# Residual added in PSUM: seeding the accumulation banks of a feed-forward block from ScalarE

## The chip, the cores and the metric

The kernel runs on one core of one Trainium2 chip. The metric is the device time in microseconds (us) of one execution; the times here are the median of three runs of the kernel before, and one further execution that was taken with the hardware profiler on.

## What is computed

The reference is a small decoder trunk over 512 tokens of width 1024, in two layers. Each layer is a feed-forward block (FFN), a mixer (gated linear attention, GLA, in the first layer; stick-breaking attention, SB, in the second), and another FFN, so there are four FFNs in all:

```
x = x + 0.5 * (silu(h @ w_gate) * (h @ w_up)) @ w_down      # h = rmsnorm(x); D_FF = 2816
x = x + mixer(rmsnorm(x))
x = x + 0.5 * (the same with the second FFN's weights)
```

The change concerns the FFNs alone: the additions of `0.5 * (...) @ w_down` to the residual `x`, and the way in which part of the gate and up products are formed.

## The kernel before

**Layout and precision.** The residual stays on the chip as eight tiles `xs[0..7]` of 128 features by 512 tokens. Every matrix factor is held as two parts, a rounded one (`wh`, `hh`, `nh` and so on) and a remainder (`wl`, `hl`, `nl`); one product is three matmuls, high by high, low by high and high by low (`mm3`, line 89; `prod`, line 523). A weight block is loaded by SyncE, rounded by ScalarE (line 133, called a cast here) and subtracted from the original by VectorE (line 134, the remainder).

**The order of the work.** The whole kernel is one list of entries (`Entry`, `Feed`, lines 116 to 178). When an entry starts, `Feed.start` first writes down the casts and remainders of the entries up to two further on, and then the entry's own body. That order of the code counts later: between two instructions of an engine that could both run, the one written first goes first. The weight halves `wh` and `wl` have four buffers each, so that a cast waits for TensorE to finish with a block.

**An FFN.** The hidden width is cut into eleven column pairs, collected in six groups (`GROUPS`, line 449). The first gate and up products are plain (`feat`, line 183). From the third or fourth column pair on, gate and up products are formed by the seven-product scheme of `seven` (line 503): 8 gate and 9 up products in each FFN, 32 and 36 in the kernel, 68 in all; each is called a seven here. A seven has two entries. `body_1` runs four products and `body_2` three, each of 12 matmuls of 256 columns. In the order of TensorE they are

```
body_1:  w   z   q   w+=          body_2:  y   q+=   o
```

where `w`, `z`, `q` are left halves of three PSUM banks and `y`, `o` are the right halves of the banks of `z` and `w`. The sums between products are made on the way out: ScalarE copies `w` to `u2` (line 563) and `q` to `c5` (line 570); VectorE adds `z` to `u2` (line 566), `y` to `u2` to give `u3` (line 582), `u3` to `c5` (line 583), `q` to `u2` (line 586) and `o` to `u3` (line 591). All of `add` is recorded at line 539. `left` and `rest` (lines 541 to 553) then apply the silu on ScalarE (gate) or multiply by the finished gate on VectorE (up), and `close` splits the result in `hh` and `hl` for the down projection.

**Down.** `down` (line 292) multiplies a group's hidden columns by `w_down`. For each of the eight feature blocks k it accumulates `nf` hidden blocks in one PSUM bank `ps_d` (12 matmuls of 512 columns for `nf` = 4; 6 for the fifth group, which has `nf` = 2), and VectorE takes `0.5 * ps_d + x` to `x` (line 308). Entries of `down` for a group are placed between the sevens of the next group, mostly two feature blocks at a time (four for the fifth group). In the steady part one `body_1`, one `body_2` and one entry of `down` follow each other. After the sixth group, `nxt` prepares the next norm; in the last FFN the sixth group is done by `back_tok` instead. So 5 groups × 8 blocks × 4 FFNs = 160 additions are within an FFN, and 24 are in the sixth groups.

**Banks.** PSUM has eight banks, under the tags a (2), z (3), t (2) and o (1). A call of `psum` without a tag takes the next of `aazzztto` in turn (line 45).

Of the kernel before, what the change touches and what calls it, by code (L numbers as in the profile page):

```python
# [14 lines left out]
AF = mybir.ActivationFunctionType  # L15
ALU = mybir.AluOpType
# [3 lines left out]
T = 512  # L20
D = 1024
KD = D // P
# [8 lines left out]
def decoder(ctx: ExitStack, tc: tile.TileContext, a: dict, out: bass.AP):  # L31
    nc = tc.nc
# [10 lines left out]
    turn_ = [0]  # L43

    def psum(name, tag=None):
        if tag is None:
# [12 lines left out]
    xs = [xp.tile([P, T], F32, name=f"x{k}") for k in range(KD)]  # L59

    def mm(ps, l, r, first, last):
        st["pe"] = nc.tensor.matmul(ps, l, r, start=first, stop=last).ins  # L62

# [16 lines left out]
    def back_by(ps, u):  # L80
        return ps.rearrange("p (m u) -> p u m", u=u)

    def like(x, u):
        return x.rearrange("p (u m) -> p u m", u=u)

    def mm2(ps, l, r, first, last):
        mm(pairs(ps), l, two(r), first, last)

    def mm3(ps, wh, wl, mh, ml, first, last, o=pairs, m=two):
        ps, mh, ml = o(ps), m(mh), m(ml)  # L90
        mm(ps, wh, mh, first, False)
        mm(ps, wl, mh, False, False)
        mm(ps, wh, ml, False, last)
# [89 lines left out]
    def feat(ch, f, evac, tag=None, defer=None, part=KD // 2, o=pairs, m=two):  # L183


        def body(W):
            (wh, wl), = W
            ps = psum("ps_f", tag)
            for ks in (range(0, part), range(part, KD)):
                for k in ks:  # L190
                    mm3(ps, wh[:, k], wl[:, k], st["h"][k], st["l"][k], k == 0, k == KD - 1, o, m)
                if ks[-1] == KD - 1:
                    if defer is None:
                        evac(ps)
# [31 lines left out]
    def back(w, r0, nf, hs, scale, nxt, late=0, tags=(None,) * 8):  # L226


        for dh in range(2):
# [45 lines left out]
            for f0, u in units:  # L275
# [13 lines left out]

                feed.q.append(Entry([u], body))  # L290

    def down(w, r0, nf, hs, part, nxt):

        nd = KD // nf
        src = w[r0 : r0 + nf * P, part * nd * P : (part + 1) * nd * P]
        ch = Chunk(src.rearrange("(f p) c -> p f c", p=P), nf, nd * P)
        ch.few = True

        def body(W):
            (wh, wl), = W  # L300
            for m in range(nd):
                ps = psum("ps_d")
                s = slice(m * P, (m + 1) * P)
                for f in range(nf):
                    mm3(ps, wh[:, f, s], wl[:, f, s], hs[f][0], hs[f][1], f == 0, f == nf - 1)
                k = part * nd + m
                x = like(xs[k], 4)
                nc.vector.scalar_tensor_tensor(  # L308
                    out=x, in0=back_by(ps, 4), scalar=0.5, in1=x, op0=ALU.mult, op1=ALU.add
                )  # L310
                if nxt is not None:
                    nxt(k)
                yield

        feed.q.append(Entry([(ch, lambda t: t, nf, nd * P)], body))
# [26 lines left out]
    st = {}  # L342
# [99 lines left out]
    class FFN:  # L442
# [10 lines left out]
        def __init__(self, wg, wu, wd, gi, nxt, first=False, last=False):  # L453
# [6 lines left out]
            for group, (c0, c1) in enumerate(self.GROUPS):  # L460
# [29 lines left out]
                for x in downs[put:]:  # L490
                    down(*x)
# [4 lines left out]
            if last:  # L496
                back_tok(wd, c0 * 256, n, self.hs[group], nxt)
            else:
                for x in downs:
                    down(*x)  # L500
            self.total = len(feed.q) - base

        def seven(self, ch, group=None):

            H = T // 2
            s12, v = [None], {}

# [12 lines left out]
            def prod(o, w, w0, b, first=True):  # L523
                for j in range(4):
                    bh, bl = b(j)
                    wh, wl = w[0][:, w0 + j], w[1][:, w0 + j]
                    for n, (l_, r_) in enumerate(((wh, bh), (wl, bh), (wh, bl))):
                        nc.tensor.matmul(  # L528
                            pairs(o), l_, r_, start=first and j + n == 0, stop=j == 3 and n == 2, skip_group_check=True
                        )  # L530

            def half(k0, c):
                return lambda j: (four(st["h"][k0 + j])[:, c], four(st["l"][k0 + j])[:, c])

            def part(name):
                return self.tp.tile([P, H], F32, tag="c", bufs=2, name=name)

            def add(o, x, y):
                nc.vector.tensor_tensor(out=o, in0=x, in1=y, op=ALU.add)  # L539

            def left(o, w):
                if group is None:
                    nc.scalar.activation(o[:, 0:H], w, AF.Silu)
                else:
                    nc.vector.tensor_tensor(out=o[:, 0:H], in0=w, in1=self.gates[0][:, 0:H], op=ALU.mult)

            def rest(o, c):
                if group is None:
                    st["silu"] = nc.scalar.activation(o[:, c:T], o[:, c:T], AF.Silu).ins
                    self.gates.append(o)  # L550
                    return
                nc.vector.tensor_tensor(out=o[:, c:T], in0=o[:, c:T], in1=self.gates.pop(0)[:, c:T], op=ALU.mult)
                self.close(o, group)

            def body_1(W):
                ax, s = W

                v["w"], v["z"], v["q"] = psum("ps_w"), psum("ps_z"), psum("ps_q")
                w, z, q = (v[n][:, 0:H] for n in "wzq")
                v["o"] = self.tp.tile([P, T], F32, tag="t", name="o0")  # L560
                prod(w, ax, 0, half(0, 0))
                v["u2"] = part("u2")
                nc.scalar.copy(v["u2"], w)
                yield
                prod(z, s, 4, lambda j: self.t_half(1, j))
                add(v["u2"], z, v["u2"])
                yield
                prod(q, s, 0, lambda j: self.t_half(0, j))
                v["c5"] = part("c5")
                nc.scalar.copy(v["c5"], q)  # L570
                yield
                prod(w, ax, 4, half(4, 0), first=False)
                left(v["o"], w)
                yield

            def body_2(W):
                s, a22 = W
                q, y = v["q"][:, 0:H], v["z"][:, H:T]
# [672 lines left out]
    with tc.tile_pool(name="ip", bufs=1) as ip:  # L1251
# [95 lines left out]
        ps = psum("ps_g")  # L1347
# [51 lines left out]
```

## Time and profile before

| | |
|---|---|
| median of 3 runs | 1829.39 us (1829.24 to 1830.08) |
| profiled execution, own time | 1829.62 us |
| its span, first to last instruction | 1827.8 us |
| TensorE busy | 1794.6 us (98%) |
| VectorE busy | 1454.1 us (80%) |
| ScalarE busy | 935.9 us (51%) |
| granted TensorE clock | 0.997 |
| chain that ended last | PE 82%, DVE 10%, ACT 4%, DMA 3% |

In the profile PE is TensorE's matmul, PEld its weight load, DVE VectorE, ACT ScalarE, POOL GpSimd and SP SyncE. A row of a group shows line, engine and operation, output and inputs by the kernel's names, shape and count; then total busy time, the mean ns of one, and the idle time of the engine just before them with what ended it. A row of the timeline shows start in us from the span's start, duration, engine, line, and in brackets the engine's idle time before it and the releaser. A matmul's duration is its whole passage, so successive matmuls overlap; the distance of their starts is the rate.

### The profile page before, as it was taken

Reading aid. Unit: us, or ns where it says so; the run is one execution under the profiler, and the core shown is the slowest. Engines: PE = TensorE matmul, PEld = TensorE weight load, DVE = VectorE, ACT = ScalarE, POOL = GpSimd, SP = SyncE. Lnnn points to the kernel's source line nnn. Section 1 sums busy time; section 2 is a strip of 40 time slices with the busy share of each in tenths; the row PEclk is TensorE's granted clock in tenths of the full one; section 3 lists DMA queues with packets and bytes.
Section 4 is the critical chain, followed back from the end, with each engine's and each line's share of the span. In section 5 each row is a group of like instructions: output and inputs, shape, how many; then the busy total and the mean of one; then the engine's idle time right before and its main releaser. Section 6 shows DMA issues by size and latency. Waiting matters only on the chain.

```text
span 1827.8 us, 28865 instructions
## 1 busy us (share of the span) xinstructions
PE 1794.6 (98%) x11790; PEld 1642.5 (90%) x11790; DVE 1454.1 (80%) x2311; ACT 935.9 (51%) x1450; POOL 7.3 (0%) x17
## 2 busy tenths in 40 slices
PE   7999999999999999999999999999999999999998
PEld 6899999889988899999989999999888788999997
DVE  5987878775776988887889878777878769888785
ACT  5544444543664544444464444445888855444344
POOL 0000000100000000000000000000000000000000
PEclk9999999999999999999999999999999999999999
DMA  5333332322123333333234233223222222333321
GB/s 162 101 119 104 106 126 82 113 70 70 47 70 102 107 115 105 104 116 105 81 109 134 86 122 105 92 94 104 70 64 64 67 95 93 127 105 104 117 92 69
DMA packets 177511, 179.01 MB, mean 98 GB/s; under 512 B 4034, under 2 KB 167924, under 8 KB 177380
## 3 DMA queue, kind: packets, MB, share of 16 engines
q1 hardware_dynamic: 176192, 175.13, 29.7%
q8 instruction: 92, 1.51, 0.3%
q0 software_dynamic: 512, 0.99, 0.2%
q10 hardware_dynamic: 676, 1.07, 0.2%
q14 instruction: 39, 0.32, 0.1%
HBM read 175.11 MB, written 2.10 MB: 97 GB/s over the span
## 4 chain that ended last, share of the span: by engine, by line
PE 82%; DVE 10%; ACT 4%; DMA 3%; issue 1%; SPq 0%; ACTq 0%; DVEq 0%
PE ps_d L62 24%; PE ps_w L528 14%; PE ps_f L62 12%; PE ps_z L528 9%; PE ps_q L528 9%; PE ps_t L62 4%; PE ps_b L62 3%; DVE wl L134 2%; PE ps_S L62 1%; DMA raw<-in_ffn_w_up_dram 1%; PE ps_bt L62 1%; ACT wh L133 1%; PE ps_oT L1141 1%; PE ps_z L1079 1%; ACT l L439 1%
## 5 line engine op out<-in xcount | busy, mean ns | idle before, releaser
L134 DVE TENSOR_TENSOR wl<-raw,wh 128x1024 fp32r<-128x1024 f32 x244 | 261.9, 1073 | 68.2 <-ACT wh L133 67.2
L133 ACT CAST wh<-raw 128x1024 fp32r<-128x1024 f32 x244 | 225.4, 927 | 120.9 <-PE ps_f L62 42.0
L62 PE MATMUL ps_d<-hh,wh 128*128 128x512 f32 x672 | 255.0, 379 | 0.0
L62 PE MATMUL ps_d<-hl,wh 128*128 128x512 f32 x672 | 254.8, 379 | 0.0
L62 PE MATMUL ps_d<-hh,wl 128*128 128x512 f32 x672 | 254.8, 379 | 0.0
L133 ACT CAST wh<-s 128x1024 fp32r<-128x1024 f32 x136 | 142.3, 1046 | 131.9 <-PE ps_q L528 76.8
L62 PE MATMUL ps_f<-xh,wh 128*128 128x512 f32 x448 | 177.2, 396 | 5.2 <-ACT wh L133 3.7
L134 DVE TENSOR_TENSOR wl<-s,wh 128x1024 fp32r<-128x1024 f32 x136 | 166.0, 1222 | 17.8 <-ACT wh L133 16.5
L308 DVE SCALAR_TENSOR_TENSOR x<-ps_d,x 128x512 f32<-128x512 f32 x184 | 125.2, 689 | 64.5 <-PE ps_d L62 64.5
L62 PE MATMUL ps_f<-xh,wl 128*128 128x512 f32 x448 | 170.8, 381 | 0.5 <-DVE wl L134 0.5
L62 PE MATMUL ps_f<-xl,wh 128*128 128x512 f32 x448 | 170.5, 381 | 0.0
L133 ACT CAST wh<-rawd 128x1024 fp32r<-128x1024 f32 x84 | 88.0, 1048 | 136.1 <-PE ps_d L62 115.1
L528 PE MATMUL ps_z<-th,wh 128*128 128x256 f32 x544 | 150.2, 276 | 3.1 <-DVE u L539 3.1
L528 PE MATMUL ps_w<-nh,wl 128*128 128x256 f32 x544 | 149.7, 275 | 0.0
L528 PE MATMUL ps_z<-tl,wh 128*128 128x256 f32 x544 | 149.7, 275 | 0.0
L528 PE MATMUL ps_w<-nl,wh 128*128 128x256 f32 x544 | 149.7, 275 | 0.0
L528 PE MATMUL ps_z<-th,wl 128*128 128x256 f32 x544 | 149.7, 275 | 0.0
L528 PE MATMUL ps_w<-nh,wh 128*128 128x256 f32 x544 | 149.6, 275 | 0.0
L62 PEld LDWEIGHTS ps_d<-hl,wh 128*128 128x128 f32 x672 | 127.1, 189 | 17.9
L62 PEld LDWEIGHTS ps_d<-hh,wh 128*128 128x128 f32 x672 | 127.3, 189 | 16.5
L62 PEld LDWEIGHTS ps_d<-hh,wl 128*128 128x128 f32 x672 | 127.3, 189 | 16.4
L134 DVE TENSOR_TENSOR wl<-rawd,wh 128x1024 fp32r<-128x1024 f32 x84 | 102.8, 1224 | 38.3 <-ACT wh L133 38.0
(250 smaller groups left out, 4707.1 us busy)
## 6 DMA issues: line engine op xcount, KB each, us to landing
raw<-in_ffn_w_gate_dram SPq DMA_DIRECT2D x43, 1024.0 KB, 5.2
raw<-in_ffn_w_up_dram SPq DMA_DIRECT2D x43, 1024.0 KB, 5.2
rawd<-in_ffn_w_down_dram SPq DMA_DIRECT2D x84, 512.0 KB, 3.4
raw<-in_gla_w_in_dram SPq DMA_DIRECT2D x12, 1024.0 KB, 5.2
raw<-in_sb_w_in_dram SPq DMA_DIRECT2D x16, 512.0 KB, 3.7
raw<-in_gla_w_out_dram SPq DMA_DIRECT2D x4, 1024.0 KB, 4.9
raw<-in_sb_w_in_dram SPq DMA_DIRECT2D x4, 1024.0 KB, 5.0
raw<-in_sb_w_out_dram SPq DMA_DIRECT2D x4, 1024.0 KB, 4.9
```

Of the source, the lines that this page charges most:

```text
L62: st["pe"] = nc.tensor.matmul(ps, l, r, start=first, stop=last).ins
L133: nc.scalar.copy(h, r).ins,
L134: nc.vector.tensor_tensor(out=l, in0=r, in1=h.bitcast(F32), op=ALU.subtract).ins,
L308: nc.vector.scalar_tensor_tensor(out=x, in0=back_by(ps, 4), scalar=0.5, in1=x, op0=ALU.mult, op1=ALU.add)
L439: st["last"] = nc.scalar.activation(o, i, fn, **kw).ins
L528: nc.tensor.matmul(pairs(o), l_, r_, start=first and j + n == 0, stop=j == 3 and n == 2, skip_group_check=True)
L1079: nc.tensor.matmul(o_, l_, r_, start=first, stop=last, skip_group_check=True)
L1141: nc.tensor.matmul(po[e * 64 : e * 64 + 64, j * P : T], self.v[j][:, c : c + 64], self.wt[p, e][bk][:, c0 : c0 + n], start=j == 0, stop=j ...
```

## The change

Three things are done.

- `down`, in the first five groups of an FFN: before the matmuls of block k, ScalarE writes twice the residual, `2 * x`, in the bank (`seed`). The matmuls add to it, none of them with the start flag. ScalarE reads the bank back at half scale, `x = 0.5 * ps`, in place of VectorE's multiply-and-add. The seed of block k+1 is written down after the first of the `nf` hidden blocks of block k; that of block 0 at the head of the group's first entry. The sixth group keeps the old way.
- Banks: `down` uses the two banks with tag a alone; the sevens use the other six in the order `zzztto`. The rest still goes through `aazzztto`.
- `seven`: ScalarE copies the first product `w` into the bank of `z`, and four products are added there one after the other, with ScalarE and VectorE reading the sum in between. The order on TensorE becomes

```
body_1:  w   q   z+=   w+=        body_2:  z+=   q+=   z+=
```

with ScalarE's copy of `w` to `z` after the first, of `q` to `c5` after the second, of `z` to `u2` after the third; and VectorE's `z + c5` after the first product of `body_2`. Three VectorE additions of each seven go (`u2`, `u3`, and `o` to `u3`).

```diff
+        if tag == "s":
+            tag = "zzztto"[turn_[1] % 6]
+            turn_[1] += 1
...
+        def seed(k):
+            seeds[k] = psum("ps_d", "a")
+            nc.scalar.activation(
+                seeds[k].rearrange("p (m u) -> p m u", u=4),
+                xs[k].rearrange("p (u m) -> p m u", u=4),
+                AF.Copy,
+                scale=2.0,
+            )
+
         def body(W):
             (wh, wl), = W
+            if nxt is None and part == 0:
+                seed(0)
             for m in range(nd):
-                ps = psum("ps_d")
+                k = part * nd + m
                 s = slice(m * P, (m + 1) * P)
+                seeded = nxt is None
+                ps = seeds.pop(k) if seeded else psum("ps_d", "a")
                 for f in range(nf):
-                    mm3(ps, wh[:, f, s], wl[:, f, s], hs[f][0], hs[f][1], f == 0, f == nf - 1)
-                k = part * nd + m
+                    mm3(ps, wh[:, f, s], wl[:, f, s], hs[f][0], hs[f][1], not seeded and f == 0, f == nf - 1)
+                    if seeded and f == 0 and k + 1 < KD:
+                        seed(k + 1)
                 x = like(xs[k], 4)
-                nc.vector.scalar_tensor_tensor(
-                    out=x, in0=back_by(ps, 4), scalar=0.5, in1=x, op0=ALU.mult, op1=ALU.add
-                )
-                if nxt is not None:
+                if seeded:
+                    nc.scalar.activation(x, back_by(ps, 4), AF.Copy, scale=0.5)
+                else:
+                    nc.vector.scalar_tensor_tensor(
+                        out=x, in0=back_by(ps, 4), scalar=0.5, in1=x, op0=ALU.mult, op1=ALU.add
+                    )
                     nxt(k)
...
                 prod(w, ax, 0, half(0, 0))
-                v["u2"] = part("u2")
-                nc.scalar.copy(v["u2"], w)
-                yield
-                prod(z, s, 4, lambda j: self.t_half(1, j))
-                add(v["u2"], z, v["u2"])
+                nc.scalar.copy(z, w)
                 yield
                 prod(q, s, 0, lambda j: self.t_half(0, j))
                 v["c5"] = part("c5")
                 nc.scalar.copy(v["c5"], q)
                 yield
+                prod(z, s, 4, lambda j: self.t_half(1, j), first=False)
+                v["u2"] = part("u2")
+                nc.scalar.copy(v["u2"], z)
+                yield
                 prod(w, ax, 4, half(4, 0), first=False)
                 left(v["o"], w)
...
-                prod(y, s, 0, lambda j: self.t_half(2, j))
-                u3 = o1[:, 0:H]
-                add(u3, y, v["u2"])
-                nc.vector.tensor_tensor(out=o1[:, H:T], in0=u3, in1=v["c5"], op=ALU.add)
+                prod(z, s, 0, lambda j: self.t_half(2, j), first=False)
+                add(o1[:, H:T], z, v["c5"])
                 yield
                 prod(q, s, 4, half(4, 1), first=False)
                 add(o0[:, H:T], q, v["u2"])
                 rest(o0, H)
                 yield
-                o = v["w"][:, H:T]
-                prod(o, a22, 0, lambda j: self.t_half(3, j))
-                add(o1[:, 0:H], o, u3)
-                rest(o1, 0)
+                prod(z, a22, 0, lambda j: self.t_half(3, j), first=False)
+                left(o1, z)
+                rest(o1, H)
                 yield
```

More of the change, by code (lines that the diff above doesn't have):

```diff
@@ L42, in decoder @@
     order = "aazzztto"
-    turn_ = [0]
+    turn_ = [0, 0]
     def psum(name, tag=None):
-        if tag is None:
+        if tag == "s":
+            tag = "zzztto"[turn_[1] % 6]
+            turn_[1] += 1
+        elif tag is None:
             tag = order[turn_[0] % 8]
@@ L61, in mm @@
     def mm(ps, l, r, first, last):
-        st["pe"] = nc.tensor.matmul(ps, l, r, start=first, stop=last).ins
+        st["pe"] = nc.tensor.matmul(ps, l, r, start=first, stop=last, skip_group_check=True).ins
     def two(m):
@@ L290, in back @@
                 feed.q.append(Entry([u], body))
+    seeds = {}
     def down(w, r0, nf, hs, part, nxt):
@@ L556, in body_1 @@
                 ax, s = W
-                v["w"], v["z"], v["q"] = psum("ps_w"), psum("ps_z"), psum("ps_q")
-                w, z, q = (v[n][:, 0:H] for n in "wzq")
+                v["w"], v["z"], v["q"] = (psum(n, "s")[:, 0:H] for n in ("ps_w", "ps_z", "ps_q"))
+                w, z, q = (v[n] for n in "wzq")
                 v["o"] = self.tp.tile([P, T], F32, tag="t", name="o0")
                 prod(w, ax, 0, half(0, 0))
-                v["u2"] = part("u2")
-                nc.scalar.copy(v["u2"], w)
-                yield
-                prod(z, s, 4, lambda j: self.t_half(1, j))
-                add(v["u2"], z, v["u2"])
+                nc.scalar.copy(z, w)
                 yield
@@ L577, in body_2 @@
                 s, a22 = W
-                q, y = v["q"][:, 0:H], v["z"][:, H:T]
+                q, z = v["q"], v["z"]
                 o0, o1 = v["o"], self.tp.tile([P, T], F32, tag="t", name="o1")
-                prod(y, s, 0, lambda j: self.t_half(2, j))
-                u3 = o1[:, 0:H]
-                add(u3, y, v["u2"])
-                nc.vector.tensor_tensor(out=o1[:, H:T], in0=u3, in1=v["c5"], op=ALU.add)
+                prod(z, s, 0, lambda j: self.t_half(2, j), first=False)
+                add(o1[:, H:T], z, v["c5"])
                 yield
```

## The prediction

> **What bounds the kernel now.** I read the page first, then the groups of instructions by form, TensorE's waits, and at last the timeline of two neighbouring sevens in the steady part of the first FFN.
>
> ```profile
> span 1827.8 us, 28865 instructions
> PE 1794.6 (98%) x11790; PEld 1642.5 (90%) x11790; DVE 1454.1 (80%) x2311; ACT 935.9 (51%) x1450; POOL 7.3 (0%) x17
> PEclk9999999999999999999999999999999999999999
> ```
>
> TensorE is busy for 98% at the full granted clock. The change keeps every matmul, so only TensorE's waits can be won. Those that end in the instructions that the change touches are two lines of the waits:
>
> ```profile
> PE ps_z L528 <- DVE u L539: 3.1, 5, 1.4
> PE ps_w L528 <- DVE o L545: 0.7, 2, 0.3
> ```
>
> That is 3.1 + 0.7 = 3.8 us in the whole kernel, and it bounds the gain. VectorE at 80% looks like a load worth lifting, but almost nobody waits for it here. So the question is which new waits TensorE gets.
>
> **Engine time moved.** The rows that price it:
>
> ```profile
> L308 DVE SCALAR_TENSOR_TENSOR x<-ps_d,x 128x512 f32<-128x512 f32 x184 | 125.2, 689 | 64.5 <-PE ps_d L62 64.5
> L539 DVE TENSOR_TENSOR u<-ps_z,u 128x256 f32<-128x256 f32 x68 | 28.6, 421 | 11.1 <-PE ps_z L528 11.1
> L563 ACT COPY u<-ps_w 128x256 f32<-128x256 f32 x68 | 25.3, 372 | 18.5 <-PE ps_w L528 18.5
> L1228 ACT ACTIVATE ps_bt<-x 128x512 f32<-128x512 f32 x8 | 4.8, 602 | 8.2 <-DVE x L1223 8.2
> L1150 ACT CAST oh<-ps_oT 128x512 fp32r<-128x512 f32 x8 | 4.7, 586 | 10.4 <-PE ps_oT L1141 10.4
> ```
>
> VectorE loses 160 × 0.689 = 110 us of residual additions and 3 × 68 × 0.421 = 86 us of half-width additions: 1454 − 196 = 1258 us, 69%. (The last `left` and `rest` of a seven work on two halves instead of one whole, which moves either engine by some 5 us and is left out.) ScalarE gains 160 seeds at 0.602 (the nearest row that writes a bank), 160 read-backs at 0.586 (one that reads a bank) and 68 copies at 0.372: 190 + 25 = 215, so 936 + 215 = 1151 us, 63%. Neither becomes the bound by its total. What decides is the order of reads and writes in one bank.
>
> **The seven, the new wait.** In `body_2` the three products are now z+=, q+=, z+=. VectorE must read z between the first and the third, so it has as long as the second takes. Before, the same read (`u3`, of y) stood at the same place of the code, and nobody waited for it: the third product went to another bank. So the trace shows when VectorE gets there. An up seven, then a gate seven, on TensorE (first matmul of `body_2`, last of its first product, first of its third):
>
> ```profile
> 206.28 0.28 PE L528 MATMUL ps_z<-th,wh 128*128 128x256 f32 x1
> ...
> 207.51 0.28 PE L528 MATMUL ps_z<-tl,wh 128*128 128x256 f32 x1
> ...
> 208.96 0.28 PE L528 MATMUL ps_w<-th,wh 128*128 128x256 f32 x1
> ...
> 222.07 0.28 PE L528 MATMUL ps_z<-tl,wh 128*128 128x256 f32 x1
> ...
> 223.52 0.28 PE L528 MATMUL ps_w<-th,wh 128*128 128x256 f32 x1
> ```
>
> and on VectorE:
>
> ```profile
> 206.55 1.22 DVE L134 TENSOR_TENSOR wl<-raw,wh 128x1024 fp32r<-128x1024 f32 x1 [0.21 <-ACT wh L133]
> 207.69 0.42 DVE L545 TENSOR_TENSOR o<-ps_w,o 128x256 f32<-128x256 f32 x1
> 208.03 1.22 DVE L134 TENSOR_TENSOR wl<-s,wh 128x1024 fp32r<-128x1024 f32 x1
> 209.16 0.42 DVE L539 TENSOR_TENSOR o<-ps_z,u 128x256 f32<-128x256 f32 x1
> ...
> 221.22 1.22 DVE L134 TENSOR_TENSOR wl<-raw,wh 128x1024 fp32r<-128x1024 f32 x1
> 222.39 1.23 DVE L134 TENSOR_TENSOR wl<-s,wh 128x1024 fp32r<-128x1024 f32 x1
> 223.53 0.42 DVE L539 TENSOR_TENSOR o<-ps_z,u 128x256 f32<-128x256 f32 x1
> ```
>
> In the up seven the first product is complete at 207.51 + 0.28 = 207.79, but at 208.03 VectorE takes a remainder of 1.22 us, because the code writes the next seven's split ahead of this body. The read ends at 209.16 + 0.42 = 209.58, while the third product started at 208.96. With both on one bank the third product waits. How long a restart takes is shown by the one large wait of this kind:
>
> ```profile
> 162.03 0.42 DVE L539 TENSOR_TENSOR u<-ps_z,u 128x256 f32<-128x256 f32 x1
> 162.50 0.38 PE L528 MATMUL ps_z<-th,wh 128*128 128x256 f32 x1 [1.42 <-DVE u L539]
> ```
>
> 162.50 − 162.45 = 0.05. So the up seven would wait 209.58 + 0.05 − 208.96 = 0.67 us, the gate seven 223.53 + 0.42 + 0.05 − 223.52 = 0.48.
>
> Does VectorE, relieved, get there earlier? The two remainders come when ScalarE has cast, and that hangs on TensorE:
>
> ```profile
> 205.20 0.37 ACT L570 COPY c<-ps_q 128x256 f32<-128x256 f32 x1 [2.36 <-PE ps_q L528]
> 205.47 1.05 ACT L133 CAST wh<-raw 128x1024 fp32r<-128x1024 f32 x1
> 206.48 1.05 ACT L133 CAST wh<-s 128x1024 fp32r<-128x1024 f32 x1
> ...
> 221.04 0.38 ACT L543 ACTIVATE o<-ps_w 128x256 f32<-128x256 f32 x1
> 221.32 1.04 ACT L133 CAST wh<-s 128x1024 fp32r<-128x1024 f32 x1
> ```
>
> The chain starts with the copy at the end of the third product of `body_1` (that of z to `u2` now takes the place of that of q), and the cast behind it needs the buffer that this product frees. So copy, cast, remainder, remainder come at the same distance as before, and the additions that VectorE loses do not lie in that chain. I therefore take the waits at their full size: 36 × 0.67 + 32 × 0.48 = 24.1 + 15.4 = 39.5 us. The bounds are 0 (the read goes ahead of the second remainder: see the rivals) and 39.5 plus what the first two sevens of each FFN wait beyond it, where VectorE is further behind; I take 39.5, which counts those sevens like the others.
>
> The two ScalarE steps in `body_1` I take at nothing. The copy of w to z has a product of cover (12 matmuls: 207.62 − 206.28 = 1.34 by 208.96 − 206.28 = 2.68 for 24): 1.34 − 0.16 of tail − 0.37 − 2 × 0.05 = 0.7 us to spare, and ScalarE now waits for w there (18.5 us over 68 copies). That of z to `u2` has the same cover, w+=. Behind a cast of 1.05 us each would cost some 0.3; if all 136 did, 41 us, an end that the idle half of ScalarE speaks against.
>
> **Down.** Two rows of the chain and one group give TensorE's side:
>
> ```profile
> 199.79 1.29 PE ps_d L62 x6
> ...
> 303.01 5.18 PE ps_d L62 x24
> ```
> ```profile
> L62 PE MATMUL ps_d<-hh,wh 128*128 128x512 f32 x672 | 255.0, 379 | 0.0
> ```
>
> Seed and read-back of one bank are 0.586 + 0.602 = 1.19 us; with the matmuls' tail (0.379 of passage less 1.29 / 6 = 0.215 of rate: 0.16) and two hand-overs of 0.05 the bank is ready 1.45 us after its product's last issue. The other bank covers this with one block: 12 matmuls, twice the 1.29 us below = 2.59 us, for `nf` = 4, so a cast of 1.05 still fits and the price is nothing. In the fifth group a block takes half, 1.29 us, and 1.45 does not fit. ScalarE has other work in that entry:
>
> ```profile
> 303.15 0.62 ACT L614 CAST hh<-o 128x512 fp32r<-128x512 f32 x1 [0.34 <-DVE o L552]
> ...
> 306.42 0.62 ACT L614 CAST hh<-o 128x512 fp32r<-128x512 f32 x1 [2.13 <-DVE o L552]
> ```
>
> Two of the four blocks of an entry are affected (the first two are seeded in the pause before), in two entries of four FFNs: 16 blocks, each between 0.16 and, with a split of the seven before it in the way as at 306.42 (the entry is the second row of the chain, from 303.0 to 308.2), 0.78 us: 2.6 to 12.5. I take 5. Seeds of block 0 (20 of them) need a bank and an `x` that have been ready for microseconds, and ScalarE has gaps like the 2.36 us above: nothing. The sixth groups keep VectorE's addition but have two banks instead of eight; in the page's order VectorE has 2.59 us for a 0.689 us step that comes first in the code: nothing, at most some tenths of a us.
>
> **Sum.** 1829.6 (the profiled execution; the median of 1829.4 is 0.2 below) + 39.5 for the sevens + 5 for the fifth groups − 3.8 for the old waits, whose VectorE reads (`u2`, and `left` ahead of `o` in w's bank) no longer stand between two products = 1870.3, or 1870 on the median.
>
> **Rivals.**
> *The read is in time: no change, or a little faster.* The point is sharp: the third product is unhurt if VectorE's read ends by 208.91, so starts by 208.49. VectorE is free at 208.03; if the read went ahead of the second remainder, it would end at 208.45. For it: the compiler may order anew, and in the gate seven the remainder began only 0.04 us after the product's end (222.35 against 222.39). Against it: both sevens shown have the remainder first. If only the gate sevens escape: 1829.6 + 24.1 + 5 − 3.8 = 1855. If all do: 1829.6 − 3.8 = 1825.8, or with the fifth groups' 5 us 1831.
> *Seeds come late.* If the seed of block 0 is only reached in its place of the code, behind the casts (1.05) and the silu of the seven before it (two of 0.38), each of 20 costs some 0.2 + 0.76 + 1.05 + 0.60 = 2.6 us: 52 us more, 1922.
> *TensorE's clock falls.* The new waits make short pauses regular. In the trace pauses do not lower the clock: between 1420 and 1440 us TensorE was busy for 18.74 of 20 us at a clock of 1.00.
>
> ```profile
> 1420.00:1440.00 20.00, 18.74 (x105) 13.83 (x104) 16.31 (x25) 18.50 (x42) 0.00 (x0) 1.00 0.24 87
> ```
>
> If it ran at half rate for one product after each of 68 waits, 68 × 1.34 = 91 us would come on top: 1961. The Trainium skill, "TensorE: Matmul & The Clock Gate", section "A second HAM failure mode: psum-queue depth-cycling", says that frequent small pauses between groups of matmuls, made by waiting for banks, can make the clock gate swing between half and full. By that rule this change would cost the 91 us; the window above speaks against it.
>
> **How the numbers follow.** Under 0.2% (3.7 us) a change of this kernel can hardly be told from none. Both kinds of seven wait: 0.55, 1870 (its own range 1858 to 1884). Only a part of them waits: 0.20, near 1855. Seeds late: 0.04, 1922. Clock: 0.01, 1961. No wait, and the fifth groups' price eats the gain: 0.13, within 0.2%. No wait and the 3.8 us won: 0.07, 1826. Slower is 0.55 + 0.20 + 0.04 + 0.01 = 0.80. The range from 1828 to 1890 leaves out the last case, half of the one before and the late seeds and the clock: 0.07 + 0.06 + 0.05 = 0.18.
>
> **What would show it.** Right: the waits of TensorE get a line of `ps_z` at line 528 behind VectorE's addition with about 68 counts and some 35 to 45 us, 0.67 and 0.48 each; the period of seven, seven's second entry and down grows from 14.56 us (223.52 − 208.96) to about 15.1; VectorE falls to some 1258 us busy, ScalarE rises to some 1151; small waits of `ps_d` for ScalarE in the fifth groups only. Wrong: no such line and a period of 14.56; or waits of `ps_d` behind the seed at the head of each group; or granted clock below 1.00 in the steady part.

## The result and the profile after

The changed kernel takes 1901.84 us (median of 4 runs, 1900.56 to 1904.51), the kernel before 1829.32 in the same sitting: 1.0397 times as long (95% interval 1.0385 to 1.041). The profiled execution took 1904.51 us. So the change costs 72.5 us, where 40 were forecast; the direction was right, the size was not, and the time lies above the forecast's range of 1828 to 1890.

The page of the changed kernel, its span, its engines and the granted clock:

```profile
span 1902.7 us, 28753 instructions
...
PE 1836.2 (97%) x11790; PEld 1642.8 (86%) x11790; DVE 1289.5 (68%) x1983; ACT 1209.5 (64%) x1872; POOL 7.3 (0%) x17
...
PEclk9999999999999999999999999999999999999999
...
PE 55%; DVE 21%; ACT 18%; DMA 4%; issue 3%; SPq 0%; ACTq 0%; DVEq 0%
```

The span grew by 74.9 us. Weight loads are as long as before (1642.8 against 1642.5), their count and the matmuls' count are the same, and the granted clock is at 90% or more in all forty slices (the digit 9), 0.998 over the run. So TensorE does the same work and waits more. The fourth part says who it waits for: in the chain that ended last PE fell from 82% to 55%, VectorE rose from 10% to 21%, ScalarE from 4% to 18%. Both engines are less than 70% busy, and still they hold the chain.

The waits of TensorE's weight loads name the places (us in total, times, longest). Each stage begins with a weight load, so this view shows waits that the matmul rows hide:

```profile
PEld ps_z L549 <- DVE o L560: 36.2, 68, 2.3
PEld ps_d L65 <- ACT ps_d L306: 20.5, 30, 2.7
PEld ps_z L549 <- ACT ps_z L583: 10.8, 27, 0.4
PEld ps_d L65 <- ACT wh L136: 10.4, 22, 0.5
```

Together 77.9 us, against 74.9 of growth. A wait of a weight load is not yet lost time, since matmuls issued before it may still be running. By the distances of matmul starts the four places lose 25.1, 14.4, 9.8 and 9.8 us, and the matmuls right behind them some 15 more (last section). In the kernel before the same view had two lines at these places, which are gone:

```profile
PEld ps_z L528 <- DVE u L539: 4.1, 5, 1.6
...
PEld ps_w L528 <- DVE o L545: 1.0, 2, 0.5
```

The first line of after is the forecast one: all 68 sevens, 36.2 us, the third product of `body_2` behind VectorE's read of z. The other three, 41.7 us, were forecast at 5. Where they come from is seen first in the groups of ScalarE, the seed, the read-back and the new copy:

```profile
L306 ACT ACTIVATE ps_d<-x 128x512 f32<-128x512 f32 x160 | 174.9, 1093 | 2.5
...
L328 ACT ACTIVATE x<-ps_d 128x512 f32<-128x512 f32 x160 | 95.5, 597 | 102.1 <-PE ps_d L65 99.4
...
L583 ACT COPY ps_z<-ps_w 128x256 f32<-128x256 f32 x68 | 23.5, 345 | 2.8 <-PE ps_w L549 2.6
```

The read-back takes 597 ns (forecast 586). The seed takes 1093 ns, not 602: it handles the same 128 x 512 elements, but its source `xs` is read four elements at a time, each 128 further on, and it writes the bank element after element. The read-back walks the other way: it reads the bank with a step of four elements and writes `x` along the row.

What such a seed does to the sevens, on ScalarE and then on TensorE of the changed kernel (start, duration; the bracket is the idle time before and its releaser):

```profile
193.50 1.04 ACT L136 CAST wh<-rawd 128x1024 fp32r<-128x1024 f32 x1
194.44 1.11 ACT L306 ACTIVATE ps_d<-x 128x512 f32<-128x512 f32 x1
195.48 0.33 ACT L583 COPY ps_z<-ps_w 128x256 f32<-128x256 f32 x1
```

```profile
194.04 0.28 PE L549 MATMUL ps_w<-nl,wh 128*128 128x256 f32 x1
194.15 0.28 PE L549 MATMUL ps_q<-th,wh 128*128 128x256 f32 x1
...
195.86 0.38 PE L549 MATMUL ps_z<-th,wh 128*128 128x256 f32 x1 [0.21 <-ACT ps_z L583]
```

The first product `w` is complete at 194.04 + 0.28 = 194.32. ScalarE is in a cast until 194.5, takes the seed of 1.11 us next, and only then the copy of w to z. The cover of one product (1.34 us) ends at 195.49; z+= starts at 195.86.

What it does in a fifth group, where a block of `down` lasts 1.29 us (ScalarE, then TensorE):

```profile
1275.77 1.04 ACT L136 CAST wh<-rawd 128x1024 fp32r<-128x1024 f32 x1 [1.20 <-DMA rawd<-in_ffn_w_down_dram]
1276.72 0.59 ACT L328 ACTIVATE x<-ps_d 128x512 f32<-128x512 f32 x1
1277.21 0.61 ACT L631 CAST hh<-o 128x512 fp32r<-128x512 f32 x1
1277.72 1.07 ACT L306 ACTIVATE ps_d<-x 128x512 f32<-128x512 f32 x1
```

```profile
1276.15 0.38 PE L65 MATMUL ps_d<-hl,wh 128*128 128x512 f32 x1
1278.84 0.74 PE L65 MATMUL ps_d<-hh,wh 128*128 128x512 f32 x1 [2.32 <-ACT ps_d L306]
1279.38 0.63 PE L65 MATMUL ps_d<-hh,wl 128*128 128x512 f32 x1
```

Cast, read-back, cast and seed stand in one row on ScalarE, and TensorE waits for the last of them for 2.32 us. The matmuls behind it pass in 0.63 instead of 0.38 us; the last section comes back to that.

Last, a sight that no step of the prediction had. TensorE of the changed kernel around the read of a gate seven (third product of `body_2` on the last line), with VectorE's read:

```profile
201.21 0.28 PE L549 MATMUL ps_q<-nl,wh 128*128 128x256 f32 x1
201.33 0.38 PE L65 MATMUL ps_d<-hh,wh 128*128 128x512 f32 x1
201.82 0.38 PE L549 MATMUL ps_z<-th,wh 128*128 128x256 f32 x1
```

```profile
200.20 1.23 DVE L137 TENSOR_TENSOR wl<-s,wh 128x1024 fp32r<-128x1024 f32 x1
201.34 0.42 DVE L560 TENSOR_TENSOR o<-ps_z,c 128x256 f32<-128x256 f32 x1
```

VectorE's order is as forecast, remainder first, read second. But a matmul of `down` (line 65) stands between q+= and the third product, where the code has it later: the compiler filled the pause. From its start to the third product pass 0.49 us instead of 0.216, so 0.27 us are lost there and not 0.48. In an up seven two such matmuls stand there. The same freedom also costs: a matmul of `down` is put between the first two products of a seven, where its block is not yet cast (ScalarE, then TensorE):

```profile
208.92 1.04 ACT L136 CAST wh<-rawd 128x1024 fp32r<-128x1024 f32 x1
```

```profile
209.45 0.28 PE L549 MATMUL ps_w<-nl,wh 128*128 128x256 f32 x1
210.01 0.48 PE L65 MATMUL ps_d<-hh,wh 128*128 128x512 f32 x1 [0.28 <-ACT wh L136]
210.33 0.27 PE L549 MATMUL ps_q<-th,wh 128*128 128x256 f32 x1
```

That is one of the 22 waits of the fourth line above.

### The profile page after: what moved, and what is told of

It reads as the page before. It is cut to its first block, busy times and chain, and to the rows that moved or that the text cites. A ratio compares the mean times of both kernels' runs of the same rounds, so it can differ in the third digit from the quotient of the medians.

```text
span 1902.7 us, 28753 instructions
## 1 busy us (share of the span) xinstructions
PE 1836.2 (97%) x11790; PEld 1642.8 (86%) x11790; DVE 1289.5 (68%) x1983; ACT 1209.5 (64%) x1872; POOL 7.3 (0%) x17
## 3 DMA queue, kind: packets, MB, share of 16 engines
q1 hardware_dynamic: 176192, 175.13, 28.6%
## 4 chain that ended last, share of the span: by engine, by line
PE 55%; DVE 21%; ACT 18%; DMA 4%; issue 3%; SPq 0%; ACTq 0%; DVEq 0%
PE ps_d L65 19%; PE ps_z L549 10%; DVE wl L137 9%; ACT wh L136 8%; PE ps_f L65 8%; PE ps_t L65 4%; PE ps_q L549 3%; PE ps_b L65 3%; ACT ps_d L306 2%; DMA raw<-in_ffn_w_up_dram 2%; ACT x L328 2%; PE ps_S L65 1%; DVE o L560 1%; PE ps_bt L65 1%; PE ps_w L549 1%
## 5 line engine op out<-in xcount | busy, mean ns | idle before, releaser
L65 PE MATMUL ps_d<-hh,wh 128*128 128x512 f32 x672 | 261.2, 389 | 15.7 <-ACT ps_d L306 8.7
L549 PE MATMUL ps_z<-th,wh 128*128 128x256 f32 x816 | 234.1, 287 | 19.4 <-DVE o L560 8.5
L549 PE MATMUL ps_z<-th,wl 128*128 128x256 f32 x816 | 224.4, 275 | 0.0
L549 PE MATMUL ps_z<-tl,wh 128*128 128x256 f32 x816 | 224.4, 275 | 0.0
L549 PEld LDWEIGHTS ps_z<-th,wh 128*128 128x128 f32 x816 | 156.1, 191 | 47.0 <-DVE o L560 36.2
L306 ACT ACTIVATE ps_d<-x 128x512 f32<-128x512 f32 x160 | 174.9, 1093 | 2.5
L65 PEld LDWEIGHTS ps_d<-hh,wh 128*128 128x128 f32 x672 | 127.4, 190 | 46.5 <-ACT ps_d L306 20.5
L328 ACT ACTIVATE x<-ps_d 128x512 f32<-128x512 f32 x160 | 95.5, 597 | 102.1 <-PE ps_d L65 99.4
L549 PEld LDWEIGHTS ps_z<-tl,wh 128*128 128x128 f32 x816 | 156.7, 192 | 0.0
L549 PEld LDWEIGHTS ps_z<-th,wl 128*128 128x128 f32 x816 | 156.4, 192 | 0.0
```

Of the source, the lines that this page charges most:

```text
L306: nc.scalar.activation(seeds[k].rearrange("p (m u) -> p m u", u=4), xs[k].rearrange("p (u m) -> p m u", u=4), AF.Copy, scale=2.0,)
L328: nc.scalar.activation(x, back_by(ps, 4), AF.Copy, scale=0.5)
L549: nc.tensor.matmul(pairs(o), l_, r_, start=first and j + n == 0, stop=j == 3 and n == 2, skip_group_check=True)
```

## The experiments

The theory after the result had two parts: the wait for VectorE's read, as forecast, and ScalarE being late because the seed's walk costs nearly twice its price. The rivals: the two banks left to `down` cost by themselves, whoever adds; the rest arises only where both halves of the change meet; and the read alone is worth more than its line of waits says.

| kernel | time, us | ratio to before (95%) |
|---|---|---|
| the change | 1901.84 | 1.0397 (1.0385 to 1.041) |
| e1, seed walks rows | 1886.09 | 1.0307 (1.0292 to 1.0323) |
| e2, down's half alone | 1858.69 | 1.0157 (1.0141 to 1.0172) |
| e3, sevens' half alone | 1867.82 | 1.0206 (1.0189 to 1.0223) |
| e4, new banks alone | 1845.32 | 1.0088 (1.0073 to 1.0103) |
| e5, e1 and read before split | 1884.88 | 1.0299 (1.0278 to 1.032) |
| e6, e1 and matmuls in code order | 1876.17 | 1.0252 (1.0237 to 1.0268) |
| e7, e5 and e6 together | 1873.64 | 1.0235 (1.0212 to 1.0258) |
| e8, e7 and three banks for down | 1869.42 | 1.0215 (1.0199 to 1.023) |
| e9, e7, read first only ahead of down | 1859.21 | 1.0157 (1.014 to 1.0174) |
| e10, e2 and seed in rows | 1845.44 | 1.0087 (1.0071 to 1.0103) |
| e11, e4 and three banks | 1834.59 | 1.0024 (1.0014 to 1.0034) |
| e12, e9 and three banks | 1853.98 | 1.0129 (1.0114 to 1.0144) |

Before took 1829.8 to 1830.3 us in these sittings.

**e1: the seed in rows.** The same values go into the same places; only the order in which ScalarE walks them is that of the read-back.

```diff
-            nc.scalar.activation(
-                seeds[k].rearrange("p (m u) -> p m u", u=4),
-                xs[k].rearrange("p (u m) -> p m u", u=4),
-                AF.Copy,
-                scale=2.0,
-            )
+            nc.scalar.activation(back_by(seeds[k], 4), like(xs[k], 4), AF.Copy, scale=2.0)
```

> The whole change, but each seed walks x in rows of 128 neighbouring elements and writes its bank with a step of four, instead of reading x in runs of four at a distance of 128. Theory S (the seed's price comes from the walk through x): one seed falls from 1.09 us to about 0.60, as in the read-back; TensorE's 29 us of waits at the down products and 13 us at the third product of the seven shrink to a few us, those at the seventh product stay at about 31; time 1860 to 1872. Rival L (ScalarE is late because of the number of its steps): some 5 to 10 us come back, 1892 to 1898. Rival W (writing a bank costs this much): the seed stays at 1.09 and the time at 1902.

The group of the seed in e1:

```profile
L306 ACT ACTIVATE ps_d<-x 128x512 f32<-128x512 f32 x160 | 96.4, 602 | 2.5
```

602 ns, exactly the price that the prediction had taken from a row that writes a bank and reads its source along the row. That row writes its bank in order, as the seed of the change does, so of the two walks that the edit alters it is the one through the source that made the 1093. Two of the waits of weight loads shrink with it, from 20.5 and 10.8:

```profile
PEld ps_z L544 <- DVE o L555: 42.3, 68, 2.5
PEld ps_d L65 <- ACT wh L136: 10.4, 22, 0.5
...
PEld ps_d L65 <- ACT ps_d L306: 5.5, 8, 1.6
...
PEld ps_z L544 <- ACT ps_z L578: 0.4, 1, 0.4
```

But the time fell by 15.8 us, not by the 30 and more that the theory of the walk gave: the read's line grew by 6.1 while those two shrank by 25.4, and the profiled execution has two more stretches of half clock than the changed kernel's (last section), 1.7 us each. The walk explains half of what the forecast missed.

**e2: down's half alone.** The sevens are those of before, on the new banks.

```diff
-                v["w"], v["z"], v["q"] = (psum(n, "s")[:, 0:H] for n in ("ps_w", "ps_z", "ps_q"))
-                w, z, q = (v[n] for n in "wzq")
+                v["w"], v["z"], v["q"] = (psum(n, "s") for n in ("ps_w", "ps_z", "ps_q"))
+                w, z, q = (v[n][:, 0:H] for n in "wzq")
...
-                nc.scalar.copy(z, w)
+                v["u2"] = part("u2")
+                nc.scalar.copy(v["u2"], w)
...
```

> Down seeded and read back by ScalarE as in the change, the sevens as before but in the six banks of the change. Theory S: the waits of TensorE at the down products stay for the most part (15 to 29 us), those at the third and seventh product of a seven go; 1846 to 1862. Rival Z (the sevens' shared bank makes nearly all of the loss, and the waits at the down products are only pushed there by it): 1829 to 1836.

Its largest wait of weight loads that the change touches:

```profile
PEld ps_d L65 <- ACT ps_d L306: 26.0, 36, 2.9
```

28.6 us above before. The changed kernel's waits in the sevens, behind the read and behind the copy of w, are not there; an old one grew, the line of `ps_w` behind VectorE's `o`, from 1.0 us in 2 waits to 5.0 in 12.

**e3: the sevens' half alone.** `down` adds on VectorE as before, in its two banks.

```diff
-            if nxt is None and part == 0:
-                seed(0)
...
-                seeded = nxt is None
+                seeded = False
...
```

> The sevens as in the change, down's addition on VectorE as before but in two banks. Theory S: only the seventh product waits, behind VectorE's reading of z, 30 to 40 us; 1856 to 1866. Rival Z: 1890 to 1900. Rival N (no wait is left once ScalarE has no seeds, since the order of the instructions changes with them): 1829 to 1836.

The same view of e3:

```profile
PEld ps_z L548 <- DVE o L559: 36.3, 68, 2.4
...
PEld ps_d L65 <- DVE x L328: 5.2, 9, 1.6
```

The read's line is the changed kernel's to a tenth (36.3 against 36.2), so relieving VectorE of `down` bought it nothing, as the prediction had argued. In the second line VectorE's addition is late for the bank. The time lies 2 us above the expected range.

**e4: the banks alone.** Both arithmetics are those of before; only the tags differ (the edits of e2 and e3 together).

> Only the banks of the change: down has two banks, the sevens the other six, all arithmetic as before. Both theories: the banks cost nothing or some tenths of a us in the sixth groups, 1828 to 1832. If two banks for down are what TensorE waits for, over 1840.

1845.32 us: the two banks cost 15 us with no seed and no new order in the sevens, where some tenths were expected. Their wait, the two waits in the sevens that the kernel before has too, and a place in the timeline of e4 (VectorE, then TensorE):

```profile
PEld ps_d L65 <- DVE x L328: 14.0, 18, 1.7
...
PEld ps_z L548 <- DVE u L559: 3.1, 4, 0.8
...
PEld ps_w L548 <- DVE o L565: 1.5, 3, 0.5
```

```profile
331.58 1.28 DVE L328 SCALAR_TENSOR_TENSOR x<-ps_d,x 128x512 f32<-128x512 f32 x2
```

```profile
332.32 0.48 PE L65 MATMUL ps_d<-hh,wh 128*128 128x512 f32 x1 [0.77 <-DVE x L328]
```

This is a fifth group. Two additions leave VectorE back to back from 331.58 (the row holds two, 1.28 us together), behind a split of the hidden columns that came first, so the first bank is released at about 332.2. Before, with eight banks in turn, such a delay reached nobody. By the distances of matmul starts the fifth groups lose 7.3 us and the first group of each FFN 4.9, once in each at its third block (102.80, for example), where VectorE has sums and remainders of weight blocks ahead of the additions. The sixth groups lose 0.3.

**e5: the read first.** On top of e1, the splits that an entry writes ahead, and the loads with them, are written behind VectorE's read in the second entry of each seven.

```diff
+        def after_read(self, i, body):
+            next(body)
+            with tc.issue_after(st["read"]):
+                self.ahead(i)
+            yield
+            yield from body
...
```

> On the seeds in rows (1886 us): in the second entry of each seven the split of the next entries is written down behind VectorE's reading of z, and its VectorE part is queued behind that reading. Theory R (the third product waits because the remainder of 1.22 us stands ahead of the reading): its 39 us of waits fall to under 8, the steady sevens to none; 1846 to 1856. Rival B (VectorE or ScalarE is late anyway, and the wait only moves to another product): 1875 to 1890.

The waits of weight loads in e5:

```profile
PEld ps_q L558 <- DVE wl L138: 10.8, 8, 1.4
PEld ps_q L558 <- ACT wh L137: 9.3, 12, 0.9
...
PEld ps_z L558 <- DVE o L611: 4.3, 5, 1.4
```

The wait behind the read falls from 42.3 to 4.3 us, and the time by 1.2, less than the executions of either kernel differ. Where two sevens follow each other without a `down` between them, the split that now comes later is the one that the next seven needs: 20.1 us of waits at q take the place. The copy of w to z waits for 6.9 us instead of 0.4, and half clock comes four times instead of three. The expectation of 1846 to 1856 failed: in this order most of the wait moved and did not go.

**e6: TensorE in the order of the code.** On top of e1, every matmul of `down` is queued behind the last product written.

```diff
-                    mm3(ps, wh[:, f, s], wl[:, f, s], hs[f][0], hs[f][1], not seeded and f == 0, f == nf - 1)
+                    with tc.issue_after(st["sv"]):
+                        mm3(ps, wh[:, f, s], wl[:, f, s], hs[f][0], hs[f][1], not seeded and f == 0, f == nf - 1)
...
```

> On the seeds in rows (1886 us): the first matmuls of an entry of down are queued behind the last product of the seven before it, so that none stands between w and q. Theory H (one such matmul, put ahead by the compiler, waits there for a cast that comes late): the 22 waits of about 0.45 us plus a restart go, 12 to 16 us, but the seventh product waits some 5 to 10 longer without the matmuls that filled its pause; 1876 to 1884. Rival G (q would have waited at that place in any case): 1886 to 1896.

9.9 us less than e1, as expected; the line of `ps_d` behind the cast (22 times, 10.4 us) is gone. So the matmuls moved ahead did cost more between the first two products than they gave in the pause before the third. By the distances of matmul starts the 22 places lose 9.8 us less, and the third products 34 us instead of 31. Both terms are smaller than expected, and the profiled execution of e6 also has two stretches of half clock fewer than that of e1, so some of the 9.9 may be clock.

**e7: e5 and e6 together.**

> Both of the last two edits on the seeds in rows. Theory (R and H add): what is left are two banks for down and the starts of the FFNs; 1836 to 1846. If one of them only moves its wait: 1850 to 1875.

1873.64: the wait has only moved, as the second case of the expectation has it. The q lines of e5 stand as they were, 10.9 and 9.3 us in the same view. Of the four executions two took 1868.5 and 1870.5 us at a granted clock of 0.997 and 0.998, the other two 1876.8 and 1877.0 at 0.992; the median lies between the pairs.

**e8: e7 and three banks for down,** five for the sevens.

```diff
-            tag = "zzztto"[turn_[1] % 6]
+            tag = "zzztt"[turn_[1] % 5]
             turn_[1] += 1
+        elif tag == "d":
+            tag = "aao"[turn_[2] % 3]
+            turn_[2] += 1
...
```

> As the run with both edits, but down has three banks in turn and the sevens five. If two banks are what is left: 5 to 10 us less than with both edits, 1830 to 1838, at about the time before. If five banks are too few for the sevens: more than with both edits, at their first product.

The median is 4.2 us below e7, but e8's executions, 1868.2 to 1870.6 us, lie among those of e7, so by itself this is not clear of noise; the expected 1830 to 1838 failed. The line of `ps_d` behind the seed falls from 7.4 us to 1.0, the q lines stay.

**e9: e7, the read first only where an entry of down follows.** There the late split has `down`'s time to be made in.

```diff
-            if not e.late:
+            if not e.late or not self.q[i + 1].units[0][0].few:
                 self.ahead(i)
                 return e.body(e.W)
```

> As the run with both edits (1874 us), but the split goes behind the reading only where the entry after the seven is one of down; where a seven follows at once, the order is that of the change. Theory R (the third product's wait is the remainder ahead of the reading; the 23 us at q in the run with both edits come from weights that the edit itself made late for a seven that follows at once): the waits at q go, some 5 to 10 us at the seventh product return; 1852 to 1862. Rival B (VectorE and ScalarE are late in any order): within 5 us of 1874.

```profile
PEld ps_z L559 <- DVE o L612: 14.7, 17, 2.4
```

1859.21, 14.4 us less than e7, or 9 to 11 less than e7's two executions at the same granted clock. The q lines are gone, and the read's wait is left in 17 sevens of 68. Twelve of them are those that the next seven follows at once, with 10.7 of the 14.7 us; the other five, the gate seven of the fifth group in each FFN and the last seven, waited in e5 already. That confirms the reading of e5, and it shows that part of the read's wait could be removed and not only moved.

**e10: e2 with the seed in rows** (the edit of e1).

> Down alone as in the change (1859 us with the sevens of before), with the seeds in rows. Theory S: the seed's walk costs 10 to 14 us there and the rest of that kernel's loss is the two banks, which cost 15 with VectorE's addition too; 1844 to 1850. Rival: the seeds themselves cost, whatever their walk, over 1853.

1845.44, the time of e4 (1845.32). Seeding and reading back on ScalarE, with a seed of 602 ns, thus costs nothing that shows beyond what the two banks cost with VectorE's addition (each time is known to some 3 us by its interval); the walk costs 1858.69 − 1845.44 = 13.2 us.

**e11: e4 with three banks for down** (the edit of e8).

> All arithmetic as before, down with three banks in turn and the sevens with five. If the 15 us of the kernel with the banks of the change alone come from two banks for down: 1830 to 1835. If they come from the banks of the other products: unchanged, about 1845.

1834.59: 10.7 of the 15 us were the second bank too few. The other 4 to 5 remain; whether they come from five banks for the sevens wasn't tried.

**e12: everything mended,** e9 with three banks.

> Seeds in rows, reading first ahead of an entry of down, code order on TensorE, three banks for down. If the four causes are all: what is left are the back-to-back sevens and the starts of the FFNs, 1842 to 1855, still slower than before, since the kernel before had only 3.8 us of waits to give.

1853.98, 24 us above before. What it still waits for is the read in the 17 sevens, 15.5 us, the copy of w to z, 6.1 us in 21 waits, and what the banks cost in e11.

No version of the change that was tried beats the kernel before.

**What the runs add up to.** Banks 15.3 us (e4 against before), the sevens on those banks 1867.82 − 1845.32 = 22.5, the seed's walk 13.2, seeding as such 0: 51 of the 72.5 us. The 22.5 is a net: on e4's banks the sevens' half adds the read's wait and removes others, at the banks of `down` (14.0 to 5.2 us in the views above) and in the sevens (3.1 and 1.5). The other 21.5 appear only where both halves are in one kernel. Known of these: 9.9 for the matmuls of `down` put ahead of their cast (e6; no such line stands in e2 or e3), about 3 more for the walk when the sevens share ScalarE with it (15.8 against 13.2). No run settles the remaining 9. The profiled executions show two places for them: by the distances of matmul starts the third products lose 31 us in e1 and 25 in e3, and half clock comes three times in e1 and once in e3.

## Why the prediction was right and wrong

**Right: nothing to gain, and the wait that decides.** It argued that TensorE's waits at the touched places are the bound of any gain (3.8 us), that lifting VectorE's load would not shorten the new wait, and that the third product of `body_2` would wait for VectorE behind a remainder. The row has the 68 counts and 36.2 us (forecast 68 and 39.5), and the timeline has VectorE's remainder ahead of the read. That the totals are so near is partly luck. In the steady part an up seven waits 0.47 us and a gate seven 0.40, or 0.29 where a seven follows at once (forecast 0.67 and 0.48), and the first seven of each FFN 1.50 to 2.35, which the forecast counted like the others.

**Right in the row, too large in the time: 39.5 us for the sevens.** In e3 the third products lose 25 us by the distances of matmul starts, and the matmuls right behind them 7: 32 in all. (The 22.5 of e3 against e4 is less, since there old waits go with it.) The step took the whole wait for lost time; the compiler lays one or two matmuls of `down` in the pause, so 0.27 is lost ahead of the third product in the gate seven shown, and 0.1 behind it, instead of 0.48. Two successive periods in the steady part of the changed kernel, from third product to third product, are 14.99 and 15.87:

```profile
186.83 0.38 PE L549 MATMUL ps_z<-th,wh 128*128 128x256 f32 x1
...
201.82 0.38 PE L549 MATMUL ps_z<-th,wh 128*128 128x256 f32 x1
...
217.69 0.38 PE L549 MATMUL ps_z<-th,wh 128*128 128x256 f32 x1
```

Their mean, 15.43, is 0.87 above the 14.56 of before (forecast: about 15.1). More is lost in a period than the read's wait, which is the next steps' part.

**Wrong: the seed at 0.602, "the nearest row that writes a bank".** That row reads its source along the row. The seed doesn't, and costs 1.093; e1 gives the 0.602 back by the walk alone. What failed was the choice of the row: it fitted in engine, shape and target and was not compared in the walk through the source, which the diff shows in its `rearrange`. Three further numbers hang on it. ScalarE's total, forecast at 1151, is 1209.5, and 1133.2 in e1. (VectorE's, forecast at 1258, is 1289.5: neighbouring rows overlap, in e4 one of 0.68 us at 328.64 by 0.08 with the next at 329.24, so count times mean overstates what busy time goes.) The copy of w to z "at nothing" became 10.8 us in 27 waits, and 0.4 in e1: 0.7 us to spare was enough against a step of 0.6, not against one of 1.1. And the fifth groups, 5 us forecast within 2.6 to 12.5, lost 12.7 by the distances of matmul starts outside half clock; in e10 with row seeds they lost 6.3. They lost it in the third and fourth block of an entry, as the forecast had it. The method there was good, its input was not.

**Wrong: the two banks, priced in the fifth groups alone.** They cost 15.3 us with the old arithmetic (e4), 10.7 of them by the lack of a third (e11). "Nothing, at most some tenths of a us" was said of the sixth groups and came true there (0.3 us in e4, 0.2 in the changed kernel). For groups of four hidden blocks the prediction set the price at nothing, because 2.59 us of the other bank cover a read-back, a seed and a cast. The first group of each FFN broke that, 4.9 us in e4 and 3.8 in e10: the engine that releases the bank had other work ahead of it. The prediction also treated the banks as an attribute of the seeds, while they are an edit of their own with a price of its own.

**Missing: what the compiler does with the new pauses.** The sum assumed TensorE in the order of the code. Matmuls of `down` were moved up into the sevens, and where their cast was late TensorE waited for it, 22 times; the order of the code gives back 9.9 us (e6).

**The rivals.** The read in time did not occur. Late seeds at block 0 did not occur either: no wait over 0.2 us at a head of a group is laid to them; but the chain of ScalarE steps that this rival named (a cast, another, then the seed) did occur in the fifth groups, as at 1275.77. The clock did not fall at the 68 waits of the changed kernel: after the longest, 2.16 us at 1020.07, it is 1.00. It did fall in e1 after three such waits of about 2 us, for 3.41 us each. The rule of the Trainium skill, "TensorE: Matmul & The Clock Gate", section "A second HAM failure mode: psum-queue depth-cycling", by which the frequent small pauses would have cost 91 us, is not borne out by this kernel: the mean granted clock of the run is 0.998, as against 0.997 before. In e5, where a pause of 0.59 us and one of 1.21 stand close together at q, the clock fell four times and its mean is 0.994.

## What to carry to other kernels

Price an added step by a row that matches it in the walk of both operands, not only in engine, shape and target: the same ScalarE copy cost 602 or 1093 ns by the order in which it read its source. Count every change of the number of banks as an edit by itself, and set each stage's blocks against the latest release of the bank. A wait that is removed by order alone can come back at the next place that was covered until then, as from e1 to e5, so ask of every such wait what the step moved behind it holds up.

## What the runs showed of the hardware

**The walk through the source.** On ScalarE, 128 x 512 in four-byte floats from `xs` on the chip to a bank: 1093 ns when the source is read in runs of four elements 128 apart and the bank written in order, 602 ns when the source is read along the row and the bank written with a step of four elements; the read-back, which reads the bank with that step, takes 597 ns. So a step of four elements in the bank cost nothing that shows, and one of 128 in the source nearly doubled the time. The runs change side and length of the step together, and don't tell which of the two decides.

**Half clock after a pause.** After the 2.32 us of wait at 1278.84 the matmuls start 0.43 apart instead of 0.215. The windows of the changed kernel (us, PE, PEld, DVE, ACT, POOL, granted clock, DMA share, GB/s) show why:

```profile
1276.00:1279.00 3.00, 0.68 (x4) 0.28 (x3) 1.83 (x2) 3.00 (x5) 0.00 (x0) 0.99 0.03 9
1279.00:1282.00 3.00, 3.00 (x8) 2.34 (x9) 0.00 (x0) 1.61 (x3) 0.00 (x0) 0.50 0.00 0
```

The granted clock is 0.50 for 3.41 us, worth 1.7 us. Between the first 40 us and the last 6 of a profiled execution this comes once in the changed kernel, three times in e1, after waits of 2.27, 2.24 and 1.96 us, and never in before. The Trainium skill, "TensorE: Matmul & The Clock Gate", section "HAM oscillation — how this bites in real kernels", gives as its rule that TensorE should have no idle gaps above some 3.4 us. Here shorter ones were enough, yet the length alone does not decide: waits of 1.94 and 2.16 us in the changed kernel and of 2.49 in e2 left the clock at full, and so did this one in e6, the longest in the middle of any run:

```profile
1008.61 0.38 PE L545 MATMUL ps_z<-th,wh 128*128 128x256 f32 x1 [2.77 <-DVE o L556]
```

The granted clock is 1.00 over the 5 us behind it. What else decides, these runs don't show.

**The first matmul after a wait.** A matmul of 256 columns passes in 0.38 us behind a wait and in 0.28 in a row of its like (201.82 and 201.21 above), and its successor starts 0.22 after it instead of 0.11 (195.86, then 196.08). So each of these waits costs 0.1 us beyond its own length, as it already did at 162.50 in the kernel before.
